# A trainium kernel's tensor-engine order in three mixers: a planner with lanes for the other engines, and high weight parts used before low

## The chip, the cores and the metric

The kernel runs on one core of a Trainium2 chip. The metric is the device time of one execution in microseconds (us); smaller is better. Engines are named as in the profile: PE (TensorE), DVE (VectorE), ACT (ScalarE), POOL (GpSimd), SP (SyncE, which here only issues transfers); "ACTq" and the like are the engines' queues of DMA issues.

## The reference, cut to what matters

512 tokens of 1024 features go through two blocks. The first block has two layers, each a "hybrid mixer" (a gated delta rule, forgetting attention, pooling) and then a feed-forward part: dense in layer 0, eight experts with two per token in layer 1. The second block mixes by RWKV-7 and an RG-LRU, and ends with cross attention on a memory and a convolutional feed-forward part.

```python
for layer in range(2):                                     # first block
    h = rmsnorm(x, norm1[layer])
    x = x + hybrid_mixer(h, w_in[layer], ..., w_out[layer])
    h = rmsnorm(x, norm2[layer])
    x = x + (swiglu(h, ...) if layer == 0 else moe_swiglu(h, router[0], ...))
...
h = rms_norm(x, norm_mix_g)                                # second block
proj = h @ w_in + b_in
y_a = rwkv7_branch(proj[..., :cb0], ...) @ w_branch_a      # chunked delta rule
y_b = rglru_branch(proj[..., cb0:cb1], proj[..., cb1:cb2], ...) @ w_branch_b
x = x + (sigmoid(proj[..., cb2:cg1]) * y_a + sigmoid(proj[..., cg1:]) * y_b) @ w_mix_out
x = x + cross_attention(rms_norm(x, norm_x_g), rms_norm(mem, norm_mem_g), ...)
x = x + conv_ffn(rms_norm(x, norm_ffn_g), ...)
return rms_norm(x, norm_final_g)
```

## The kernel before

By the trace the stages lie one after another: mixer 0 (0 to 340 us), dense feed-forward (to 674), mixer 1 (to about 1050, with the routing at its end), experts (to about 1712), the second block's mixer `mix2` (to about 2200), cross attention and the last feed-forward part (to 2720). Tokens lie along the free axis, features on partitions.

A dense product of two fp32 tensors is made of three fast products. A weight block `raw` is fetched on SP's queue; ACT rounds it to `whi`, DVE (or POOL, where the list of blocks says so) makes the rest `wlo`; activations are split in the same way (`xsh`, `xsl`). PE then adds high x high, high x low and low x high into one PSUM bank. In the three mixers `glin` does this for a block of eight 128-row pieces: before, piece by piece, in the order (whi,xsh), (whi,xsl), (wlo,xsh), with a point after each three at which another strand may go on. In the text a "dense row" is one such matmul.

The order of PE's instructions in the three mixers is found by `Fibers` when the program is built. Each strand of work is a generator ("fiber") with a rank: scans and normalisation have low ranks, `dense` has 3 and is the filler. At each `yield` a fiber says what it waits for: a number of us, a PSUM bank by name (`"pm"`, `"pf"`, `"px"`), or an event. `Fibers.run` steps its own clock by a cost for each matmul and takes the ready fiber of lowest rank; when a recent-load measure is low, all ranks from 2 up are taken before the rest. The order that it finds is kept on PE; PE then executes strictly in it, and waits wherever data are late. The other engines' order is made by the framework, and their times are in the planner only as the numbers written at the yields, `rel(tag, us)` (a bank comes free so long after now) and `done(us, name)`.

Places named later:

- `tinv` inverts the 64x64 triangular chunk matrices: 15 pairs of steps on DVE (`ipr`, `Tl`, L477 and L478), two 32x32 transposes on DVE (`T`, L481; `U`, L482), then chains of 32x32 matmuls on PE, of which `px<-T,MQ` is the first. Its waits before are `yield 0.9 + 0.006*i*i` for a step and 1.5 after the transposes.
- `rwkv(j)` of `mix2` prepares two heads: `G`, `BK`, `kk`, `rk` on DVE and POOL, and on PE `px<-G,BK` and the transposes `px<-cst,BK` (the last ones stand ahead of the inverse). `scan` then goes through eight chunks (`SV`), ends with a normalisation (`rr`, L1645) and the branch outputs `yah`, `yal`.
- `rstd` sums squares over partitions (`nacc`), takes a root on ACT, and spreads the result by `rdg`. In `mix2` it waits 14.0 us at its start.
- `conv` (L673, `cy`), `gates` (`gq`, `gsl`) and the bank evictions (`raw` L670, `pr` L1289, `MQ` L910) are DVE's part of the mixers' fronts; `attend` (`fF`, `fo`, `fP`) is the attention.
- `rows` (L1844) of mixer 1 turns the normalised tokens round (`px<-cst,xg`), copies them to `hTM` on ACT (L1858) and writes them to the DRAM buffer `hd` (L1861). `mem_k` beside it makes dense products of 256 columns (`pm<-msk,whi`) for the cross attention. The experts begin with POOL's gathers of rows of `hd` (`xa`, `xb`, L1936), which PE transposes (`px<-cst,xa`).

```python
    def rows(self):
...
                self.nc.scalar.activation(hT[:, 512 * b:512 * b + 512], ps, AF.Copy, scale=self.hrms[:, n:n + 1])
                F.rel("px", 0.8)
                yield 0.3
            self.nc.scalar.dma_start(self.hd[128 * n:128 * n + 128], hT)
```

## Time and profile before

| | |
|---|---|
| runs | 2723.54, 2724.38, 2728.06 us; median 2724.38 us |
| profiled execution | 2721.48 us, of which the trace's span is 2719.6 us |
| PE busy | 2586.2 us, 95% of the span |
| DVE, ACT, POOL busy | 1576.6, 1124.7, 374.2 us |
| mean granted PE clock | 0.974 |

PE is the busiest engine by far, so what another engine does costs time only where PE waits for it. A view by stages shows where PE is not busy; a view of waits says for whom; a timeline of one engine shows when the thing waited for was made. The granted clock is given as a share of full speed: 1.00 is 2.4 GHz, and the lower level is 1.2 GHz, so that a stretch with 0.9 had a part of its time at the lower level.

### The profile page before, as it was taken

What the parts mean: (1) busy time and instruction counts of PE and PEld (TensorE: products, weight loads), DVE (VectorE), ACT (ScalarE), POOL (GpSimd) and SP (SyncE); (2) the same over time, 40 slices, a digit from 0 to 9 for tenths busy, and PEclk for the clock granted to TensorE, in tenths of its full rate; (3) what the DMA queues carried; (4) which work ended last, traced back from release to release, by engine and by line L of the source; (5) the groups of instructions that cost most, each with busy time, mean ns of one, the idle gap of its engine ahead of it and who ended that gap; (6) DMA issues with size and microseconds to landing.
All of it is one profiled execution on the core that took longest, in us unless ns stands there. A gap on an engine that the chain in (4) does not pass through costs nothing.

```text
span 2719.6 us, 43763 instructions
## 1 busy us (share of the span) xinstructions
PE 2586.2 (95%) x18022; PEld 1996.7 (73%) x18022; DVE 1576.6 (58%) x2263; ACT 1124.7 (41%) x1600; POOL 374.2 (14%) x294
## 2 busy tenths in 40 slices
PE   7999999999989998999999998799989999999997
PEld 6787788888878667777777776566666676788885
DVE  5856643434585655666666665566743644544554
ACT  5344422223434434555555554464322334433232
POOL 4332000000333311000000001143432000000000
PEclk9999999999999999999999999899989999999998
DMA  3111222223312226787777776423232521222222
GB/s 115 55 57 43 91 92 95 93 93 101 102 55 64 72 80 250 249 297 277 278 269 266 263 254 227 135 67 108 84 115 88 173 90 43 93 94 93 93 93 79
DMA packets 101424, 359.38 MB, mean 132 GB/s; under 512 B 12256, under 2 KB 15712, under 8 KB 101216
## 3 DMA queue, kind: packets, MB, share of 16 engines
q1 hardware_dynamic: 82656, 308.47, 34.0%
q0 software_dynamic: 7808, 26.22, 2.8%
q10 hardware_dynamic: 10752, 21.81, 2.2%
q8 instruction: 144, 2.36, 0.4%
q14 instruction: 64, 0.52, 0.1%
HBM read 331.28 MB, written 25.17 MB: 131 GB/s over the span
## 4 chain that ended last, share of the span: by engine, by line
PE 55%; DVE 8%; DMA 3%; issue 3%; ACT 2%; POOL 0%; ACTq 0%; DVEq 0%; POOLq 0%; SPq 0%
PE pm L278 34%; PE pf L278 10%; PE px L278 10%; DMA raw<-in_s_gu_dram 1%; PE px L282 1%; DVE ipr L477 1%; DVE wl L1962 0%; DVE cy L673 0%; DVE G L1519 0%; PE pf L282 0%; ACT wh L1961 0%; DMA ye<-y 0%; DVE wlo L398 0%; DVE Tl L478 0%; DVE SV L1613 0%
## 5 line engine op out<-in xcount | busy, mean ns | idle before, releaser
L396 ACT ACTIVATE whi<-raw 128x1024 fp32r<-128x1024 f32 (+5 forms) x310 | 302.7, 977 | 797.2 <-PE pm L278 575.2
L278 PE MATMUL pm<-xsh,whi 128*128 128x512 f32 x1280 | 531.5, 415 | 12.3 <-ACT xsh L371 6.5
L278 PE MATMUL pm<-xsh,wlo 128*128 128x512 f32 x1280 | 511.9, 400 | 2.7 <-POOL wlo L398 2.6
L278 PE MATMUL pm<-xsl,whi 128*128 128x512 f32 x1280 | 512.3, 400 | 1.3 <-DVE xsl L372 1.3
L1962 DVE TENSOR_TENSOR wl<-raw,wh 128x1536 fp32r<-128x1536 f32 (+1 forms) x224 | 341.5, 1528 | 193.1 <-PE pf L278 85.8
L1961 ACT ACTIVATE wh<-raw 128x1536 fp32r<-128x1536 f32 (+1 forms) x224 | 291.3, 1305 | 256.8 <-PE pf L278 118.1
L278 PEld LDWEIGHTS pm<-xsh,whi 128*128 128x128 f32 x1280 | 245.2, 192 | 89.2 <-issue 19.4
L398 DVE TENSOR_TENSOR wlo<-raw,whi 128x1024 fp32r<-128x1024 f32 (+5 forms) x236 | 257.5, 1092 | 64.8 <-ACT whi L396 64.4
L278 PEld LDWEIGHTS pm<-xsh,wlo 128*128 128x128 f32 x1280 | 244.5, 191 | 62.9 <-POOL wlo L398 5.0
L278 PEld LDWEIGHTS pm<-xsl,whi 128*128 128x128 f32 x1280 | 245.3, 192 | 60.2 <-issue 4.5
L398 POOL TENSOR_TENSOR wlo<-raw,whi 128x1024 fp32r<-128x1024 f32 x74 | 181.1, 2447 | 359.7 <-ACT whi L396 359.7
L278 PE MATMUL pm<-hidl,whi 128*128 128x512 f32 x352 | 138.9, 395 | 0.0
L278 PE MATMUL pm<-hidh,wlo 128*128 128x512 f32 x352 | 138.6, 394 | 0.0
L278 PE MATMUL pm<-hidh,whi 128*128 128x512 f32 x352 | 137.9, 393 | 0.0
L1210 DVE TENSOR_TENSOR X<-X,pm 128x512 f32<-128x512 f32 x48 | 33.0, 688 | 135.1 <-PE pm L278 135.1
L278 PE MATMUL pf<-raw,xs 128*32 128x384 f32 x1024 | 103.2, 496 | 0.0
L278 PE MATMUL pm<-wh,xh 128*128 128x384 f32 x256 | 92.0, 370 | 7.4 <-ACT wh L1961 6.0
L278 PE MATMUL pm<-wl,xh 128*128 128x384 f32 x256 | 88.0, 345 | 3.6 <-DVE wl L1962 3.5
L278 PE MATMUL pf<-wh,xl 128*128 128x384 f32 x256 | 86.1, 337 | 0.0
L278 PE MATMUL pm<-wh,xl 128*128 128x384 f32 x256 | 86.0, 337 | 0.0
L278 PE MATMUL pf<-wl,xh 128*128 128x384 f32 x256 | 85.8, 336 | 0.0
L278 PE MATMUL pf<-wh,xh 128*128 128x384 f32 x256 | 84.6, 336 | 0.0
(606 smaller groups left out, 4697.5 us busy)
## 6 DMA issues: line engine op xcount, KB each, us to landing
raw<-in_s_gu_dram SPq DMA_DIRECT2D x128, 768.0 KB, 6.3
raw<-in_s_dn_dram SPq DMA_DIRECT2D x96, 512.0 KB, 4.4
raw<-in_f_gu_dram SPq DMA_DIRECT2D x44, 512.0 KB, 3.7
raw<-in_b_gu_dram SPq DMA_DIRECT2D x44, 512.0 KB, 3.7
raw<-in_b_wi_dram SPq DMA_DIRECT2D x38, 512.0 KB, 3.9
raw<-in_wq_dram SPq DMA_DIRECT2D x28, 512.0 KB, 3.6
raw<-in_f_dn_dram SPq DMA_DIRECT2D x16, 512.0 KB, 3.6
raw<-in_b_dn_dram SPq DMA_DIRECT2D x16, 512.0 KB, 3.6
```

Of the source, the lines that this page charges most:

```text
L278: return self.nc.tensor.matmul(o, l, r, **k)
L282: return self.nc.tensor.transpose(o, a, i)
L396: nc.scalar.activation(hi, raw, AF.Copy)
L398: (eng or nc.vector).tensor_tensor(lo, raw, hi.bitcast(F32), op=ALU.subtract)
L477: nc.vector.tensor_tensor(pr, A_, T_, op=ALU.mult)
L1210: nc.vector.tensor_tensor(self.X[m], self.X[m], ps, op=ALU.add)
L1961: self.wmark = act(hi, raw, AF.Copy)
L1962: tt(lo, raw, hi.bitcast(F32), op=ALU.subtract)
```

## The change

Only the planner's numbers and the order inside `glin` are changed; the work is the same.

- `Fibers` gets a lane (a list of taken intervals) for DVE, ACT, POOL, SP and the transfers. `Watch` and `Engines` stand between the kernel and the engines, and enter each instruction on its lane with a cost by its size, after its inputs are ready and its output buffer is free. A matmul waits on the planner's clock for its inputs.
- A number at a `yield` no longer counts: any number but 0 now means "until the last work that this fiber gave to another engine is done", a transfer's landing included. `rel` and `done` take their times in the same way. A list of tiles at a `yield` waits for these. `rstd` so waits for its input `acc` itself.
- Matmuls get other costs, by type and shape.
- `glin` now issues all (whi,x high) and (whi,x low) pairs of a block first, and then the low parts in groups of two, with a point for other strands after each group only.

```diff
     def set(self, lat, *k):
-        self.event(*k).t = self.t + lat
+        if self.cur is None:
+            return
+        self.event(*k).t = max(self.t, self.cur[4]) if lat else self.t
 
     def rel(self, tag, lat=1.0):
-        self.banks.setdefault(tag, []).append(self.t + lat)
+        if self.cur is None:
+            return
+        read = self.cur[5].get(tag)
+        t = self.used[read.pop(0)] if read else self.cur[4]
+        self.banks.setdefault(tag, []).append(max(t, self.t) + self.SEM)
...
+    def place(self, lane, t, cost):
+
+        iv = self.lanes[lane]
+        k = len(iv)
+        while k and iv[k - 1][0] > t:
+            k -= 1
+        if k and iv[k - 1][1] > t:
+            t = iv[k - 1][1]
+        while k < len(iv) and iv[k][0] < t + cost:
+            t = max(t, iv[k][1])
+            k += 1
+        iv.insert(k, (t, t + cost))
...
+    def work(self, lane, cost, outs, ins, land=0.0):
+
+        t = max([self.ready.get(i, 0.0) for i in ins] +
+                [max(self.ready.get(o, 0.0), self.used.get(o, 0.0)) for o in outs] + [0.0])
+        e = self.place(lane, t, cost)
+        if land:
+            e += land
...
+        if self.cur:
+            self.cur[4] = max(self.cur[4], e + self.SEM)
...
             try:
                 w = next(f[2])
-                f[3] = w if isinstance(w, (Event, str)) else self.t + w
+                f[3] = w if isinstance(w, (Event, str, list)) else max(self.t, f[4]) if w else self.t
...
+class Watch:
+
+    FIX = {"DVE": (0.155, 0.00104), "ACT": (0.19, 0.00084), "POOL": (0.35, 0.002)}
...
+        if "dma_start" in op:
+            n = int(np.prod(out.shape)) * 4
+            F.work(self.lane, {"ACT": 0.33, "SP": 0.33, "POOL": 0.56}[self.lane], [], ins)
+            F.work("DMA", n / 290e3, outs, ins, 1.7)
+            return
+        n = max(int(np.prod(x.shape[1:])) for x in every)
+        fix, per = self.FIX[self.lane]
+        if self.lane == "DVE":
+            per *= {"reciprocal": 6, "tensor_tensor_scan": 2}.get(op, 1)
+        elif "accum_out" in k:
+            fix += 0.19
+        F.work(self.lane, fix + per * n, outs, ins)
...
     def glin(self, ps, w, acts, first=True, last=True):
+
         n = len(acts)
+        yield list(w[:1])
         for k, a in enumerate(acts):
-            self.mm3(ps, [(w[0][:, k], w[1][:, k], a[0], a[1])], first and k == 0, last and k == n - 1)
+            yield list(a)
+            self.acc(ps, [(w[0][:, k], a[0]), (w[0][:, k], a[1])], first and k == 0, False)
+        yield list(w[1:])
+        for k in range(0, n, 2):
+            self.acc(ps, [(w[1][:, j], acts[j][0]) for j in range(k, min(k + 2, n))], False, last and k + 2 >= n)
             yield 0
...
         def rstd():
-            yield 14.0
+            yield [acc]
             st["R"], _ = yield from self.rstd_(acc)
```

What the change moves on PE is shown at three places; rows ending in x8 or the like stand for so many matmuls.

**The inverse of `mix2`**, PE, before: the start of `tinv`'s matmuls (`T32` is the `T` of the text). Ahead of the first row stand 141 dense rows, and ahead of these the last transposes of `BK`.

```order
L278 MATMUL px_17524<-T32_17511,MQ_16316 32x32 x32
L278 MATMUL px_17559<-T32_17511,MQ_16618 32x32 x4
L278 MATMUL pm_17501<-xsh_15352,whi_17459 128x512
L278 MATMUL pm_17501<-xsl_15353,whi_17459 128x512
L278 MATMUL pm_17501<-xsh_15352,wlo_17462 128x512
L278 MATMUL pm_17501<-xsh_15356,whi_17459 128x512
L278 MATMUL pm_17501<-xsl_15357,whi_17459 128x512
L278 MATMUL pm_17501<-xsh_15356,wlo_17462 128x512
L278 MATMUL pm_17501<-xsh_15360,whi_17459 128x512
L278 MATMUL pm_17501<-xsl_15361,whi_17459 128x512
L278 MATMUL pm_17501<-xsh_15360,wlo_17462 128x512
L278 MATMUL px_17559<-T32_17511,MQ_16618 32x32 x24
```

The same place of the changed kernel; ahead of the first row stand 82 dense rows, back to the same transposes of `BK`.

```order
L357 MATMUL px_17441<-T32_17411,MQ_16293 32x32 x32
L357 MATMUL pm_17432<-xsh_15340,whi_17389 128x512
L357 MATMUL pm_17432<-xsl_15341,whi_17389 128x512
L357 MATMUL pm_17432<-xsh_15344,whi_17389 128x512
L357 MATMUL pm_17432<-xsl_15345,whi_17389 128x512
L357 MATMUL pm_17432<-xsh_15348,whi_17389 128x512
L357 MATMUL pm_17432<-xsl_15349,whi_17389 128x512
L357 MATMUL px_17482<-T32_17411,MQ_16595 32x32 x24
L357 MATMUL pm_17432<-xsh_15352,whi_17389 128x512
```

The inverse has moved forward past 58 of the dense rows counted from the mixer's start (from 858 to 800), and the filler between its small matmuls comes in groups of six, where it had nine. Within the whole inverse 46 dense rows are now strewn, where it was 36; the dense rows left over stand in the scan and behind it.

**The end of mixer 1**, PE, before: the routing's counts (`rsm`, `oh`), the last of the eight groups of token transposes (`xg`), and the first of the 153 rows of `mem_k` that follow up to `px<-cst,xa` of the experts.

```order
L278 MATMUL px<-rsm,oh 128x8 x8
L278 MATMUL px<-rsm,oh 32x8 x8
L282 MATMUL px<-cst,xg 128x128 x4
L278 MATMUL pm<-msk_8566,whi 128x256
L278 MATMUL pm<-msk_8567,whi 128x256
L278 MATMUL pm<-msk_8566,wlo 128x256
```

The changed kernel, from shortly before its last group of token transposes to the first transposes of the experts.

```order
L357 MATMUL pm<-msk_8461,whi 128x256
L357 MATMUL pm<-msk_8531,whi 128x256
L357 MATMUL pm<-msk_8532,whi 128x256
L361 MATMUL px<-cst,xg 128x128 x4
L357 MATMUL pm<-msk_8531,whi 128x256
L357 MATMUL pm<-msk_8532,whi 128x256
L357 MATMUL pm<-msk_8401,wlo 128x256 x2
L357 MATMUL pm<-msk_8412,wlo 128x256 x2
L357 MATMUL pm<-msk_8460,wlo 128x256 x2
L357 MATMUL pm<-msk_8531,wlo 128x256 x2
L361 MATMUL px<-cst,xa 128x128 x8
L361 MATMUL px<-cst,xb 128x32 x8
```

Before, seven of the eight groups stood three rows apart and were out 153 rows ahead of the experts. Now the groups stand 8, 28, 8, 28, 10, 26 and 10 rows apart, and from the last to the experts there are ten rows.

**The normalisation at the front of `mix2`**, PE, before: 90 dense rows stand ahead of `nacc`, and 12 between it and `rdg`.

```order
L278 MATMUL pf<-xsh,wlo 128x512
L278 MATMUL px<-cst,nacc 128x1 x4
L278 MATMUL pf<-xsh,whi 128x512
L278 MATMUL pf<-xsl,whi 128x512
L278 MATMUL pf<-xsh,wlo 128x512
```

The changed kernel, where 30 dense rows stand ahead of `nacc`.

```order
L357 MATMUL pm<-xsl,whi 128x512
L357 MATMUL pm<-xsh,wlo 128x512 x8
L357 MATMUL px<-cst,nacc 128x1 x4
L357 MATMUL px<-rdg,cst 128x512
L357 MATMUL pm<-xsh,whi 128x512
L357 MATMUL pm<-xsl,whi 128x512
```

The root's input is now summed 60 dense rows sooner, and no row is left between `nacc` and `rdg`. In mixers 0 and 1 the same strand moved from 82 to 49 dense rows after the start, with twelve still between the two.

## Rows read from the trace of the kernel before

**Rows 1.** Windows by stage: busy us (instructions) of PE, PEld, DVE, ACT, POOL; PEclk; DMA.

```profile
0.00:340.00 340.00, 308.91 (x3053) 249.20 (x3054) 222.94 (x428) 152.11 (x294) 95.65 (x75) 0.97 0.23 72
340.00:674.00 334.00, 334.00 (x1441) 270.92 (x1440) 142.04 (x166) 90.13 (x106) 0.00 (x0) 1.00 0.29 94
674.00:1050.00 376.00, 354.08 (x3285) 282.22 (x3284) 230.71 (x469) 160.49 (x308) 110.32 (x87) 0.95 0.26 82
1712.00:2200.00 488.00, 447.13 (x3741) 328.79 (x3740) 286.57 (x424) 194.64 (x284) 136.73 (x96) 0.95 0.34 106
```

**Rows 2.** Waits of PE, 1712 to 2200: waited for: us in total, times, longest.

```profile
PE px L278 <- issue: 8.8, 6, 2.7
PE px L278 <- DVE G L1520: 7.8, 8, 2.6
PE px L278 <- DVE SV L1613: 3.5, 4, 1.7
PE pm L278 <- POOL wlo L398: 2.6, 4, 0.9
```

**Rows 3.** Timeline of PE around the inverse of mix2 (start, us, line).

```profile
1968.83 0.86 PE L278 MATMUL px<-cst,BK 64*64 64x64 f32 x22
...
2006.95 0.82 PE L278 MATMUL px<-T,MQ 32*32 32x32 f32 x72
```

**Rows 4.** Timeline of DVE before the inverse of mix2.

```profile
1987.11 2.22 DVE L481 STREAM_TRANSPOSE T<-Tl 128x1024 f32<-128x1024 f32 x1
...
1989.81 1.98 DVE L482 STREAM_TRANSPOSE U<-Tl 128x1024 f32<-128x1024 f32 x1
```

**Rows 5.** Timeline of PE at the normalisation of mix2.

```profile
1751.82 0.95 PE L278 MATMUL px<-cst,nacc 128*128 128x1 f32 x8
...
1755.51 1.02 PE L278 MATMUL px<-rdg,cst 128*128 128x512 f32 x2
1757.94 0.50 PE L278 MATMUL pm<-xsh,whi 128*128 128x512 f32 x1 [1.41 <-DVE pr L1289]
```

**Rows 6.** Timeline of ACT in the gates of mixer 0.

```profile
42.31 1.28 ACT L818 ACT_TABLE_LOAD   x1
```

**Rows 7.** Windows of the attention in mixer 1.

```profile
900.00:960.00 60.00, 54.25 (x426) 38.44 (x425) 37.89 (x95) 32.35 (x82) 14.27 (x20) 0.91 0.26 82
```

**Rows 8.** Timeline of PE at the end of mixer 1.

```profile
1042.95 0.66 PE L282 MATMUL px<-cst,xg 128*128 128x128 f32 x4 [0.32 <-DVE tokens L1834]
...
1064.68 1.03 PE L282 MATMUL px<-cst,xa 128*128 128x128 f32 x8
```

**Rows 9.** Timeline of ACT after it.

```profile
1043.64 0.69 ACT L1858 ACTIVATE hTM<-px,rtm 128x512 f32<-128x512 f32 x1 [3.26 <-PE px L282]
...
1046.21 0.39 ACTq L1861 DMA_DIRECT2D hd<-hTM  x1
```

**Rows 10.** Timeline of POOL: the first gather.

```profile
1050.26 1.26 POOL L1936 DMA_INDIRECT xa<-hd,tokens  x1 [23.51 <-DVE mK L1906]
```

**Rows 11.** The tile xa: from issue to landing.

```profile
DMA to landing us min/median/max: 5.0/5.6/12.8
```

**Rows 12.** Windows at the end of mixer 1.

```profile
1020.00:1064.60 44.60, 39.53 (x292) 37.48 (x292) 23.35 (x66) 16.58 (x22) 6.46 (x6) 0.89 0.57 193
1050.00:1064.60 14.60, 13.92 (x118) 13.93 (x119) 7.13 (x9) 3.18 (x4) 3.97 (x4) 1.00 0.89 293
```

**Rows 13.** Waits of PE, 20 to 340 us.

```profile
PE px L278 <- DVE MQ L910: 4.4, 2, 3.6
PE px L278 <- DVE T L481: 1.9, 1, 1.9
```

**Rows 14.** Timeline of DVE, one operation twice, in rwkv.

```profile
1856.32 3.01 DVE L1519 SCALAR_TENSOR_TENSOR G<-kk,EE 64x504 f32<-64x504 f32 x1
...
1859.44 0.68 DVE L1519 SCALAR_TENSOR_TENSOR G<-kk,EE 64x504 f32<-64x504 f32 x1
```

**Rows 15.** Timeline of POOL in the same stretch.

```profile
1856.40 2.38 POOL L398 TENSOR_TENSOR wlo<-raw,whi 128x1024 fp32r<-128x1024 f32 x1
```

More of the change, by code (lines that the diff above doesn't have):

```diff
@@ L24 @@
 NEG = -1.0e30
+DBG = 0
 EPS = 1e-6
@@ L193 @@
 class Fibers:
-    DENSE, LO, HI = 2, 1.1, 1.5
+    DENSE, LO, HI, SEM = 2, 1.1, 1.5, 0.06
     def __init__(self, banks):
         self.t, self.n, self.q = 0.0, 0, []
-        self.heat = self.cols = self.idle = 0.0
+        self.heat = self.cols = self.idle = self.stall = 0.0
         self.tick, self.warm, self.low = 3.413, False, True
         self.banks = {k: [0.0] * v for k, v in banks.items()}
-        self.ev = {}
+        self.ev, self.ready, self.used, self.bank = {}, {}, {}, {}
+        self.lanes = {k: [] for k in ("DVE", "ACT", "POOL", "SP", "DMA")}
+        self.cur, self.plain = None, False
     def event(self, *k):
@@ L208, in set, with free, use @@
     def set(self, lat, *k):
-        self.event(*k).t = self.t + lat
+        if self.cur is None:
+            return
+        self.event(*k).t = max(self.t, self.cur[4]) if lat else self.t
     def rel(self, tag, lat=1.0):
-        self.banks.setdefault(tag, []).append(self.t + lat)
+        if self.cur is None:
[3 more added lines that the diff above has]
+        self.banks.setdefault(tag, []).append(max(t, self.t) + self.SEM)
     def add(self, gen, rank=0):
         self.n += 1
-        self.q.append([rank, self.n, gen, 0.0])
-    def use(self, us, rows):
+        self.q.append([rank, self.n, gen, 0.0, 0.0, {}])
+    def free(self, old, new):
+        self.ready[new] = max(self.ready.get(old, 0.0), self.used.get(old, 0.0))
+    def place(self, lane, t, cost):
[9 more added lines that the diff above has]
+        iv.insert(k, (t, t + cost))
+        if len(iv) > 400:
+            del iv[:200]
+        return t + cost
+    def work(self, lane, cost, outs, ins, land=0.0):
[4 more added lines that the diff above has]
+            e += land
+        for i in ins:
+            self.used[i] = max(self.used.get(i, 0.0), e)
+            if i in self.bank and self.cur:
+                read = self.cur[5].setdefault(self.bank[i], [])
+                if i not in read:
+                    read.append(i)
+        for o in outs:
+            self.ready[o] = e + self.SEM
+        if self.cur:
+            self.cur[4] = max(self.cur[4], e + self.SEM)
+    def use(self, us, rows, plain, outs, ins):
+        w = max([self.ready.get(i, 0.0) for i in ins] + [0.0]) - self.t
+        if w > 0:
+            self.stall += w
+            self.heat *= math.exp(-w / 1.7)
+            self.pass_(w)
+        if plain != self.plain:
+            us += 0.1 if plain else 0.24
+            self.plain = plain
         d = max(us * (1 if self.warm else 2), 0.036)
@@ L223, in use @@
         self.pass_(d)
+        for i in ins:
+            self.used[i] = max(self.used.get(i, 0.0), self.t)
+        for o in outs:
+            self.ready[o] = self.t + 0.2
     def pass_(self, d):
@@ L237, in _ready @@
             return min(b) if b else None
+        if isinstance(w, list):
+            return max(self.ready.get(tid(a), 0.0) for a in w)
         return w
@@ L267, in __init__, with _cost @@
         self.nc, self.F = nc, None
[L269 to L274 removed]
+    def _cost(self, o, l, r, c=4):
+        if not self.F:
+            return
+        n, m, k = int(np.prod(r.shape[1:])), int(np.prod(l.shape[1:])), r.shape[0]
+        plain = r.dtype == F32
+        if not plain:
+            ns = n * 0.453
+        else:
+            ns = n * c * 0.419
+            if k <= 32 and m <= 32:
+                ns *= 0.57
+            elif k <= 64:
+                ns *= 0.65 if n <= 64 else 0.58
+            elif m <= 64:
+                ns *= 0.89 if n <= 64 else 1.25
+            else:
+                ns = max(ns * 1.05, 54.0 * c)
+        self.F.use(ns / 1000, k / 128, plain and (k < 128 or m < 128), [tid(o)], [tid(l), tid(r)])
@@ L285, with __init__, __getattr__ @@
+class Engines:
+    def __init__(self, nc, pe):
+        self._nc = nc
+        self.vector, self.scalar = Watch(nc.vector, "DVE", pe), Watch(nc.scalar, "ACT", pe)
+        self.gpsimd, self.sync = Watch(nc.gpsimd, "POOL", pe), Watch(nc.sync, "SP", pe)
+    def __getattr__(self, n):
+        return getattr(self._nc, n)
 class Net:
     def __init__(self, tc, es, A, po):
-        self.tc, self.nc, self.A, self.po = tc, tc.nc, A, po
+        self.tc, self.A, self.po = tc, A, po
         self.pe = Tensor(tc.nc)
-        self.F = Fibers({})
+        self.nc = Engines(tc.nc, self.pe)
+        self.F, self.slots = Fibers({}), {}
@@ L690, in dense @@
                 pv.append(self.ps(tag)[:, :402])
-            yield from self.tm(2, get, acts, pv, at=lambda b, n: (b, n) == (3, 0) and done(1.5, "acc"))
+            yield from self.tm(2, get, acts, pv)
             g["pv"] = pv
@@ L1120, in mixer @@
             F.run()
+        print('model', F.t, 'idle', F.idle, 'stall', F.stall) if DBG else None
         self.pe.F = None
@@ L1127, in tm @@
             hi, lo = get()
+            yield [hi, lo]
             for n in range(len(outs)):
@@ L1282, in rstd @@
         def rstd():
-            yield 14.0
+            yield [acc]
             st["R"], _ = yield from self.rstd_(acc)
@@ L1677, in mix2 @@
             F.run()
+        print('model', F.t, 'idle', F.idle, 'stall', F.stall) if DBG else None
         self.pe.F = None
```

58 lines of the change are left out of this document (43 added, 15 removed).

## The prediction

> **What bounds the kernel now.** I read the windows by stage first. In the dense feed-forward stage PE is busy for all of its 334.00 us, with 1441 matmuls: 0.232 us for a dense row of 512 columns. In the three mixers it is not: 340 − 308.9 = 31 us idle in mixer 0, 376 − 354.1 = 22 in mixer 1, and 488 − 447.1 = 41 in mix2; the granted clock there is 0.97, 0.95 and 0.95 [rows 1]. So at most some 94 us of idle time, and what the lower clock costs, lie in the planner's reach; the rest is matmuls whose number doesn't change. A part of the 31 us is the start, where the first weights must arrive; no order helps there.
>
> The waits of PE say for whom it stands in mix2: 7.8 us for `G`, 3.5 for `SV` of the scan, 2.6 for low parts that POOL makes, and 8.8 us for nothing that the profile shows [rows 2]. Many short waits, none of them large.
>
> The other thing to see is the reverse of a wait: PE coming late to what is ready. In mix2 the last `BK` transposes start at 1968.83 and the inverse's first matmul at 2006.95 [rows 3], but DVE had `T` ready at 1987.11 + 2.22 = 1989.3, and `U` at 1989.81 + 1.98 = 1991.8 [rows 4]. The dependent chain (inverse, scan, tail) starts 15 us later than it could, and behind it filler runs short.
>
> **The change, part by part.** *The inverse of mix2.* 58 dense rows leave the stretch ahead of it: 58 × 0.232 = 13.5 us. PE would arrive at 2006.95 − 13.5 = 1993.5, 1.7 us after `U`, so the move makes no new wait by itself. It is no gain either: the 58 rows are still to be done. They pay where they stand in what was idle: in the inverse (10 more rows, 2.3 us), in the scan and its tail (48 rows, 11.1 us). Bounds: nothing, if they only push the chain along, and 13.5 us, if each finds a hole. The named holes behind the inverse are `SV`'s 3.5 us and a part of the 8.8 without a releaser; the larger ones are the half-clock stretches, which this view does not price. I take 8, above the middle, since the scan's chunks had nine dense rows each in the order and now have twelve.
>
> *The heads of mix2.* Between a head's lora product and its first `px<-G,BK` there were 33 dense rows four times; now there are 32, 36, 42 and 40. For the later three that is up to 3 + 9 + 7 = 19 rows or 4.4 us of cover, against 7.8 us of waits [rows 2]. Between 0 and 4.4 I take 3.
>
> *Low parts last.* With `wlo` used 16 rows (3.7 us) after its `whi`, instead of two, the 2.6 us for POOL's low parts [rows 2] have cover; the longest wait was 0.9. I take the whole 2.6; the low bound is nothing, if the high parts now wait instead.
>
> *The normalisation of mix2.* Before, `nacc` and `rdg` start 1751.82 and 1755.51, with twelve dense rows between them [rows 5]; now none. A table load of ACT, of which the gates of mixer 0 show one, is 1.28 us [rows 6], and the root needs one, so PE must stand between 1.28 and 1755.51 − 1751.82 = 3.7 us. I take 3, nearer to the upper end since three short operations follow the load, and give back the wait of 1.41 us for `pr`'s bank that stood right behind `rdg` [rows 5]: a loss of 1.6.
>
> Mix2 together: −8 − 3 − 2.6 + 1.6 = −12.0 us.
>
> *Attention of mixer 1.* Here PE idles 60 − 54.25 = 5.75 us, and the clock is 0.91 [rows 7], because the filler ran out. The scan starts 21 dense rows (4.9 us) earlier, and filler lasts through. Bounds 0 and 5.75; I take 4.
>
> *The end of mixer 1: a loss.* Before, the last `xg` transposes start at 1042.95, and the experts' first transposes at 1064.68 [rows 8]. In between runs a chain that nobody sees, since 153 rows of `mem_k` cover it: ACT's copy starts at 1043.64 and takes 0.69; its write `hd` is issued only at 1046.21 [rows 9], on a queue where `kd` stood before it; POOL's gather `xa` starts at 1050.26 [rows 10], 4.05 us after that issue; and a gather's landing takes 5.0 us at least, 5.6 in the median, 12.8 at most [rows 11]. From the last `xg` that makes 1.38 (to the end of the copy) + 0 to 1.88 (the queue) + 4.05 + 5.0 to 12.8 = 10.4 to 20.1 us; with 0.4 for the queue and 5.6 for the landing 11.4. Now only ten rows stand in this place, at 13.92 us for 118 of them [rows 12] 1.2 us. So 9.2 to 18.9 us lie open, most likely 10.2. PE is in order: all that follows waits. What comes back: in the 44.6 us up to the experts PE was idle 44.6 − 39.5 = 5.1 us [rows 12], mostly among the token transposes, which are now strewn with 8 to 28 rows between them. I give back 2.2 of it: a loss of 8 (4 to 19). The planner puts them so because `yield 0.3` in `rows` now waits for a landing on its clock, and it has no event from `hd` to the gathers.
>
> *The fronts of mixers 0 and 1.* `nacc` comes 33 dense rows earlier, 7.7 us, and the strands behind it too. In mixer 0 PE waited 4.4 us for `MQ` and 1.9 for `T` [rows 13]; these can go, and others come, since DVE's operations are not faster than before and PE gets to their results sooner. Without a row that decides, I take −2 for mixer 0 (it has the most idle time) and 0 for mixer 1, each with ±6.
>
> **The sum.** −12.0 − 4 + 8 − 2 = −10.0 us. The profiled execution took 2721.48 us (2719.6 of span and 1.9 around it): 2711.5. The median of the runs shown is 2.9 above it, and by that I say 2714. Against what a measurement of this kernel tells from no change, 0.2% or 5.4 us, that is faster, by not much.
>
> **The rivals.** *Lanes hurt: slower.* The lanes price a DVE instruction by its size alone. The trace shows the same `G` operation at 3.01 us and at 0.68 [rows 14]; beside the slow one POOL makes a low part, 2.38 us [rows 15]. So a planner that counts 0.68 puts PE's next step 2.33 us too early wherever such a pair meets on the chain. The place is the fronts: the inverse stands 27 rows of 256 columns earlier in mixer 0 and 51 in mixer 1, 3.2 and 6.0 us by the 0.118 us of such a row, and PE waits there for `T` already [rows 13]. If DVE's chain does not come forward, that is +9.2; with three stretched steps on it (+7.0) it outweighs the −10.0 and the time is 2724.4 − 10.0 + 16.2 = about 2731. From three such steps on this decides. For it: the mixers are where POOL works at all (96 and 110 us against 0 in the dense stage) [rows 1]. Against it: the old order, with times set by hand, has the same stretches, and DVE's work is not longer than it was. The Trainium skill ("SBUF — State Buffer", section "Who interferes with whom") says that a DVE instruction with two inputs in SBUF and a GpSimd instruction that reads SBUF take turns on a shared port pair, the later one blocked until the other ends. The trace agrees: 0.68 + 2.38 = 3.06, where 3.01 was measured. By that rule this rival is a fixed property of the lanes, not chance.
>
> *More comes than I count.* If a third of the 94 us goes, as a planner that sees all chains might bring, and the experts' start costs no more than 4, the time is 2724.4 − 31 + 4 = about 2697. For it: the low clock, which I price at nothing, has 0.05 × 488 = 24 us at full speed in mix2 alone [rows 1]. Against it: 8.8 us have no releaser, and the start of mixer 0 can't be filled.
>
> *Nothing is gained.* The stalls change their places only: filler that stands in the scan is missing elsewhere, mix2 gains some 6 instead of 12 and the experts' start takes it back: 2724.4 ± 5.4.
>
> **How the numbers follow.** The forecast, −6 to −16 us, has 0.43; more 0.14; nothing 0.19; slower 0.24. So faster 0.57, same 0.19, slower 0.24. The forecast's own range is 2708 to 2718. Eight in ten need both signs: from 2694, near the larger gain, to 2735, a little above the slower rival, since the experts' start alone can cost 11 us more than I took.
>
> **What would show it.** In the windows of the changed kernel mix2's idle time falls from 41 to about 30 us, and its inverse starts at once after `U`. In front of the first `px<-cst,xa` PE waits some 10 us, with POOL's gather the thing waited for. Waits for POOL's `wlo` are gone. In the front of mix2 one wait of about 3 us stands ahead of `rdg`. I am wrong if PE's waits for `T`, `kF` or `gq` in mixers 0 and 1 add up to more than 15 us; if `T` and `U` in mix2 come later than PE; or if the experts' start is covered after all, because the transposes come out earlier relative to the gathers than I count.

## The result

The changed kernel takes 2801.59 us (median of four runs, 2798.34 to 2804.74) against 2723.96 us before: 1.0286 times, with a 95% interval of 1.0273 to 1.0298. It is 78 us slower, where 10 us less were forecast, and lies 67 us above 2735, the upper end of the eight-in-ten range (84 us above the forecast's own 2718).

The windows view of the changed kernel, by stages (busy us and instructions of PE, PEld, DVE, ACT, POOL; granted clock; DMA). The third row ends at the experts' start, where [rows 1] ended 15 us sooner; the profiled execution took 2804.74 us, with a span of 2802.9.

```profile
0.00:374.00 374.00, 322.42 (x3055) 258.01 (x3056) 224.44 (x428) 153.83 (x294) 95.89 (x75) 0.93 0.21 65
374.00:708.00 334.00, 334.00 (x1441) 270.82 (x1440) 142.40 (x167) 90.44 (x107) 0.00 (x0) 1.00 0.29 94
708.00:1140.00 432.00, 377.51 (x3402) 302.99 (x3401) 239.58 (x478) 167.38 (x312) 114.21 (x91) 0.91 0.28 89
1786.00:2281.00 495.00, 449.80 (x3745) 329.26 (x3746) 281.00 (x429) 199.40 (x286) 134.86 (x96) 0.94 0.33 108
```

The reader is to see three things beside [rows 1]. The dense stage is the same: PE does the same 1441 matmuls in a window of 334 us and is busy throughout. Mixer 0 takes 374 us instead of 340 with practically the same matmuls (3055 against 3053); its idle time went from 31.1 to 374 − 322.4 = 51.6 us, and its busy time rose by 13.5 us too, because the clock fell from 0.97 to 0.93 (308.9 x 0.97 and 322.4 x 0.93 are both about 300). Mixer 1 up to the experts takes 432 us; before, the same work lay between 674 and 1064.68 [rows 1, 8], 391 us. Mix2, 495 against 488, has some 7 us of the loss, but 5 of them lie ahead of its first dense row, which stands 19.3 us behind the window's start, before 14.4. So 34 + 41 us lie in the two mixers for which I had set −2 − 4 + 8.

Mixer 0 in three parts of the changed kernel: the front up to the inverse's first matmuls, the inverse and the scan, and the attention.

```profile
0.00:160.00 160.00, 121.36 (x914) 100.16 (x915) 99.38 (x165) 58.59 (x88) 56.46 (x38) 0.88 0.22 72
160.00:251.00 91.00, 88.80 (x1554) 73.82 (x1553) 52.09 (x126) 41.21 (x103) 23.81 (x20) 1.00 0.19 60
251.00:301.00 50.00, 43.29 (x226) 30.63 (x226) 29.07 (x68) 22.09 (x56) 15.62 (x17) 0.93 0.07 20
```

The front of the kernel before, for the first of these rows:

```profile
0.00:160.00 160.00, 132.72 (x1278) 111.64 (x1279) 109.84 (x181) 65.34 (x104) 62.00 (x40) 0.94 0.26 82
```

The numbers of matmuls in these two rows can't be compared as they stand: the kernel before had begun its inverse at 142.6, and 304 of the 1278 are small matmuls on 32 partitions, where it is 56 of the 914. Counted in the traces, PE now does 384 dense rows in the first 160 us, where it did 500; it is idle for 38.6 us instead of 27.3, and the clock is 0.88 instead of 0.94. DVE, whose work all this waits for, does not get more done by PE's coming earlier: it is busy 99 us where it was 110.

For whom PE stands in mixer 0 of the changed kernel (us in total, times, longest):

```profile
PE px L357 <- ACT hsq L379: 6.8, 2, 4.4
PE pf L361 <- DVE fP L379: 5.7, 4, 4.7
PE pf L357 <- DVE wlo L379: 4.4, 1, 4.4
PE px L357 <- DVE kF L379: 4.4, 2, 4.2
PE px L357 <- DVE vF L379: 4.3, 2, 3.5
PE px L357 <- DVE ipr L379: 3.7, 1, 3.7
PE pm L357 <- DVE rdg L379: 3.0, 1, 3.0
```

Before, the largest were `MQ`, 4.4 [rows 13], and these two:

```profile
PE pf L278 <- DVE wlo L398: 4.4, 1, 4.4
PE px L278 <- DVE kF L666: 3.3, 1, 3.3
```

The 4.4 us for `wlo` is the same wait near the start in both kernels. The others are now waits of 3 to 7 us for each strand's next step. How one of them comes about is seen at the first `kF`. DVE, at that place:

```profile
50.07 2.41 DVE L379 COPY fxt<-nck 128x8 f32<-128x8 f32 x1
...
52.39 0.68 DVE L379 TENSOR_TENSOR raw<-pm,Rbc 128x512 f32<-128x512 f32 x1
53.94 3.95 DVE L379 SCALAR_TENSOR_TENSOR cy<-raw,par,cy 128x511 f32<-128x511 f32 x3 [0.87 <-ACT cy L379]
58.65 0.69 DVE L379 SCALAR_TENSOR_TENSOR kF<-th,cy 128x512 f32<-128x512 f32 x1 [0.76 <-ACT th L379]
```

POOL, beside it:

```profile
50.05 2.40 POOL L379 TENSOR_TENSOR wlo<-raw,whi 128x1024 fp32r<-128x1024 f32 x1
52.41 1.04 POOL L379 TENSOR_TENSOR gm<-gh,cst 128x512 f32<-128x512 f32 x1
```

PE, which had been sent for `kF`:

```profile
54.27 1.03 PE L357 MATMUL pm<-xsh,wlo 128*128 128x512 f32 x2
59.49 0.80 PE L357 MATMUL px<-cst,kF 64*64 64x64 f32 x10 [4.19 <-DVE kF L379]
```

POOL begins a low part at 50.05 that takes 2.40 us; a copy of eight columns on DVE takes 2.41 beside it; only then is the block's bank emptied (`raw`, 52.39), and `conv`'s three steps take 3.95 us together, 1.32 each, beside POOL's next operations (`kF`, a step of the same kind and size, takes 0.69 when POOL is idle). `raw`, which reads a bank in PSUM, keeps its 0.68 though POOL works. PE stands 4.19 us for `kF`. All dense rows behind this point wait with it, and these are what the next `raw`, `cy` and `vF` are made of.

In mix2 the inverse of the changed kernel: `T` and `U` on DVE, and the first of PE's matmuls for it.

```profile
2076.83 2.21 DVE L379 STREAM_TRANSPOSE T<-Tl 128x1024 f32<-128x1024 f32 x1
...
2079.51 1.98 DVE L379 STREAM_TRANSPOSE U<-Tl 128x1024 f32<-128x1024 f32 x1
```

```profile
2082.79 0.75 PE L357 MATMUL px<-T,MQ 32*32 32x32 f32 x64
```

PE comes 1.3 us after `U` (2079.51 + 1.98), as forecast. But from the stage's start (1786 for 1712) `U` is ready at 295.5, where it was at 279.8 [rows 4], 15.7 us later. Of these, 5 lie ahead of mix2's first dense row; from that row on (1805.28 for 1726.35) the chain itself is 10.8 us later. PE comes to the inverse only 3.1 us sooner, for the 13.5 us of the 58 rows taken from ahead of it, and from there to the last output product it needs 5.5 us more than before (195.1 for 189.6). PE is idle for 495 − 449.8 = 45.2 us, where I expected about 30. Some of the waits of mix2:

```profile
PE pm L357 <- DVE wlo L379: 6.4, 4, 2.9
PE pm L357 <- DVE pr L379: 6.1, 4, 1.7
PE pf L357 <- ACT ksq L379: 5.4, 4, 2.8
PE px L357 <- DVE xx L379: 4.1, 3, 1.9
PE px L357 <- DVE rdg L379: 1.6, 1, 1.6
PE px L357 <- DVE G L379: 0.8, 1, 0.8
```

`G` is down from 7.8 [rows 2] to 0.8 and POOL's low parts are gone, as I said; `rdg` costs 1.6 where I had 3. The table load that I had put between `nacc` and `rdg` starts at 1818.04, ahead of `nacc` at 1819.90 (before at 1750.05, ahead of 1751.82), and isn't in PE's wait. In their place stand DVE's `wlo`, more of `pr`, and `ksq` and `xx` (the keys' norm, and the branch with the RG-LRU), 22.0 us in the first four rows, of which `wlo` and `pr` had 1.2 and 3.7 before.

The start of the experts, on PE, ACT and POOL of the changed kernel:

```profile
1125.33 1.10 PE L357 MATMUL pm<-msk,wlo 128*128 128x256 f32 x8
1140.03 1.94 PE L361 MATMUL px<-cst,xa 128*128 128x128 f32 x8 [13.59 <-DMA xa<-hd,tokens]
```

```profile
1125.29 0.69 ACT L379 ACTIVATE hTM<-px,rtm 128x512 f32<-128x512 f32 x1 [2.81 <-PE px L361]
1126.01 0.33 ACTq L379 DMA_DIRECT2D hd<-hTM  x1
```

```profile
1130.52 1.04 POOL L379 DMA_INDIRECT xa<-hd,tokens  x1 [41.57 <-DMA hd<-hTM]
```

This is the chain of [rows 8 to 11] laid open: the last copy at 1125.29, the write at 1126.01, the gather at 1130.52 (4.51 us after; before 4.05), its data 9.4 us later (1139.89). PE waits 13.59 us.

### The profile page after: what moved, and what is told of

Read it like the earlier page. It is cut to its first block, busy times and chain, and to the rows that moved or that the text cites. A ratio compares the mean times of both kernels' runs of the same rounds, so it can differ in the third digit from the quotient of the medians.

```text
span 2802.9 us, 43777 instructions
## 1 busy us (share of the span) xinstructions
PE 2614.0 (93%) x18022; PEld 2015.6 (72%) x18022; DVE 1570.6 (56%) x2263; ACT 1134.3 (40%) x1602; POOL 372.7 (13%) x294
## 5 line engine op out<-in xcount | busy, mean ns | idle before, releaser
L357 PE MATMUL pm<-xsh,whi 128*128 128x512 f32 x1280 | 529.4, 414 | 14.4 <-ACT xsh L379 6.2
L357 PE MATMUL pm<-xsh,wlo 128*128 128x512 f32 x1280 | 451.2, 405 | 0.0
L357 PEld LDWEIGHTS pm<-xsh,whi 128*128 128x128 f32 x1280 | 247.8, 194 | 83.2 <-issue 13.5
L379 DVE TENSOR_TENSOR X<-X,pm 128x512 f32<-128x512 f32 x96 | 66.0, 687 | 218.8 <-PE pm L357 218.8
L379 DVE TENSOR_TENSOR tu<-pm,Rbc 128x512 f32<-128x512 f32 x44 | 30.4, 691 | 127.4 <-PE pm L357 127.4
L379 POOL TENSOR_TENSOR nacc<-nacc,nsq 128x512 f32<-128x512 f32 x21 | 30.6, 1456 | 516.1 <-ACT nsq L379 515.6
L379 DVE TENSOR_TENSOR tg<-pm,Rbc 128x512 f32<-128x512 f32 x44 | 30.4, 692 | 106.8 <-PE pm L357 104.3
```

The source lines that it names most:

```text
L357: return self.nc.tensor.matmul(o, l, r, **k)
L379: return f(*a, **k)
```

## The experiments

Each kernel was run with the kernel before on the same chip; ratios are to that. The table has the places in the traces that the text speaks of, in us: mixer 0's first inverse matmul (T), its scan's start and the last row of its output projection, from the span's start; the same output row and the experts' first transposes, from the end of the dense stage; and the last output product of mix2 from the experts' last product.

| kernel | ratio (95%) | m0 T | m0 scan | m0 output | m1 output | experts | mix2 |
|---|---|---|---|---|---|---|---|
| before | 1 | 142.6 | 190.2 | 327.1 | 324.1 | 366.8 | 540.5 |
| changed | 1.0286 | 158.7 | 203.9 | 355.4 | 353.6 | 408.5 | 547.9 |
| new planner in mix2 alone | 1.0003 (0.9991 to 1.0016) | 143.9 | 191.6 | 330.1 | 324.6 | 366.7 | 543.7 |
| old order of parts, lanes | 1.0229 (1.0205 to 1.0253) | 154.9 | 200.1 | 349.3 | 346.8 | 399.8 | 552.5 |
| low parts last, no lanes | 1.0024 (1.0010 to 1.0038) | 139.7 | 187.3 | 326.8 | 324.0 | 363.2 | 546.0 |
| POOL and tables priced | 1.0247 (1.0223 to 1.0271) | 156.2 | 201.9 | 340.3 | 341.1 | 395.5 | 559.1 |
| transposes without the wait | 1.0242 (1.0219 to 1.0264) | 156.0 | 201.3 | 352.4 | 353.5 | 404.4 | 545.7 |
| hand's times as floor | 1.0153 (1.0124 to 1.0183) | 142.7 | 192.3 | 339.7 | 335.4 | 391.8 | 541.5 |
| lane prices x 1.5 | 1.0118 (1.0091 to 1.0145) | 153.2 | 196.3 | 328.1 | 324.2 | 377.2 | 556.3 |
| DVE's prices x 1.5 | 1.0170 (1.0146 to 1.0195) | 180.0 | 217.2 | 339.2 | 334.8 | 385.2 | 562.1 |
| lanes in strict order | 1.0117 (1.0093 to 1.0140) | 156.4 | 201.2 | 335.1 | 329.8 | 384.3 | 539.0 |
| before, hand's times x 0.5 | 1.0329 (1.0313 to 1.0345) | 143.7 | 198.6 | 366.0 | 358.9 | 405.8 | 554.4 |
| before, hand's times x 1.5 | 1.0005 (0.9993 to 1.0017) | 153.7 | 197.8 | 325.6 | 316.6 | 357.2 | 552.4 |
| all mended | 1.0045 (1.0031 to 1.0060) | 152.6 | 195.6 | 328.3 | 323.9 | 374.9 | 536.9 |
| old planner, strict lanes in mix2 | 0.9987 (0.9976 to 0.9999) | 142.7 | 190.4 | 328.9 | 320.8 | 362.2 | 540.0 |
| the same, old order of parts | 1.0026 (1.0015 to 1.0037) | 141.7 | 187.8 | 326.3 | 323.9 | 366.4 | 552.4 |
| before, x 1.5 in mixers 0 and 1 | 0.9950 (0.9938 to 0.9962) | 153.5 | 197.6 | 325.5 | 316.5 | 357.0 | 539.8 |
| the same, strict lanes in mix2 | 0.9948 (0.9936 to 0.9960) | 156.1 | 200.2 | 328.0 | 316.9 | 358.6 | 539.7 |

Each row of places is one execution. Rows whose matmuls stand in the same order differ by up to 4.6 us (mixer 0's output 326.3 to 330.1 in the four with the old planner's order there, the experts' start 362.2 to 366.8), so a smaller difference between two rows may be chance.

**Where it is lost.** A second planner of the old kind stands beside the new one, and the two mixers take it.

```diff
-        F = self.F = self.pe.F = Fibers({"pm": 2, "pf": 3, "px": 3})
+        F = self.F = self.pe.F = Hand({"pm": 2, "pf": 3, "px": 3})
```

> Mixers 0 and 1 are planned as before the change (their matmuls stand in the old order), mix2 as after it. By the two traces mixer 0 lost 33.6 us, mixer 1 with the routing 41.7 us, and mix2 some 6 us. If the losses belong to their stages and add up: 2724 + 6 = about 2730 us. Rival: mix2 gains alone what I forecast for it (12 us) and only starts late in the changed kernel because its buffers and weights come late from before: about 2712.

2724.08 us against 2722.05: no difference, with an interval from 2 us less to 4 us more. The change to mix2 alone costs and gives nothing that can be told from this; the 78 us are lost in mixers 0 and 1, with mixer 1's end.

**The two halves of the change.** First the lanes with the old order of parts, then the new order of parts under the old planner.

```diff
-            self.acc(ps, [(w[0][:, k], a[0]), (w[0][:, k], a[1])], first and k == 0, False)
...
+            self.mm3(ps, [(w[0][:, k], w[1][:, k], a[0], a[1])], first and k == 0, last and k == n - 1)
```

> The changed planner with the old order of parts in each dense block (high, high x low, low x high, piece by piece). Theory L (the lanes price the other engines too cheaply, so PE is sent to data that are late): the order inside the blocks is not what costs, 2790 to 2810 us. Theory G (using low parts last makes the blocks longer, holds banks longer and ruins the filler): most of the 78 us comes back, 2725 to 2750.

> The kernel before with the new order inside the dense blocks alone (high parts first, then low), under the old planner. Undoing this order in the changed kernel gave 13 us back. If it costs by itself (a block's last matmuls then wait for nothing but its bank is held as long, and the filler comes in other pieces): 2730 to 2738 us. Rival: it costs only together with the lanes, where the waits for whi and wlo are planned: 2720 to 2727.

The new planner with the old order of parts: 2788.57 us, 62 us over the kernel before by the ratio, 67 by the medians. The loss is the new planner's: lanes, waits and costs of matmuls together, which no run takes apart. The order of parts has 13 of the 78 us in the changed kernel. Alone in the old kernel it costs 2727.76 against 2722.18, 1.0024 times or 6 us; I had put it down as a gain of 2.6. In its trace 5.5 us are lost in mix2 and 5.0 between mixer 0's output and the end of the dense stage. The 5.0 us stand in every run that has low parts last in mixer 0 (375.6 to 376.4 us for this stretch) and in none with the old order (370.7 to 371.1): before, five rows of the dense stage's first block stand between `nacc` and `rdg` there, with low parts last none, so that PE waits 3.0 us for `rdg` where it was 0.3, and the clock over the 20 us around it is 0.83 where it was 1.00. In mix2 the order has no fixed price: see the end of this section.

**Two prices that the lanes lack.** A DVE operation (a copy, or an operation on a tensor with a scalar or a second tensor) without an operand in PSUM waits on the planner's clock until POOL is idle; ACT pays for a new table.

```diff
+        if lock and lane == "DVE":
+            t = self.clear(t, cost)
         e = self.place(lane, t, cost)
...
+            if f in ("Exp", "Ln", "Sqrt", "Gelu_apprx_tanh", "Silu") and f != F.table:
+                F.table, fix = f, fix + 1.28
```

> The changed kernel, but on the planner's clock a DVE operation with no operand in PSUM waits until no POOL operation runs, and ACT pays 1.28 us when it changes its function table. Theory L: the front is planned nearer to what happens, and PE's extra waits for kF, hsq, vF and the T step shrink: 2740 to 2770 us. Rival (what is missing in the lanes is not these two prices, but the order in which the engines really take their work, or the loss of the margins written by hand): 2785 or more.

2791.1 us: about 10 of the 78 us. In mixers 0 and 1 the outputs came 15.1 and 12.5 us sooner, in mix2 the end came 11 us later. Up to mixer 0's output PE is idle for 37.3 us, where it was 47.9 in the changed kernel (30.1 before), but the largest waits are nearly as long as they were, some for other strands:

```profile
PE px L373 <- POOL nacc L395: 5.2, 1, 5.2
PE px L373 <- DVE ipr L395: 4.7, 1, 4.7
PE px L373 <- ACT hsq L395: 4.2, 1, 4.2
PE px L373 <- DVE MQ L395: 4.2, 1, 4.2
```

So my rival's mechanism can be a part of it, but no more; this run priced tables along with the stretch and doesn't part the two. Pricing what is known to be missing did not make the plan fit.

**The transposes at the experts' start.**

```diff
                 F.rel("px", 0.8)
-                yield 0.3
+                yield 0
```

> The changed kernel with one yield of the token transposes (rows) put back to no wait, so that they no longer wait for a transfer's landing on the planner's clock. By the trace the experts' start lost 12 us more than the part ahead of it (29.5 late at the output projection, 41.7 at the experts). If the strewn transposes are the cause: 2788 to 2794 us. Rival: the chain is as long, and other work only takes its place: 2798 to 2802.

2791.2 us: 10 us. By the table 4 of them lie at this place (from mixer 1's output to the experts 50.9 us, for 54.9 in the changed kernel; the four with the old order have 41.4 to 42.7) and 3 in mixer 0, whose order is the same. Between the last transposes and the experts there are 112 rows now instead of ten, and still PE waits 9.42 us. ACT's last write, POOL's gather, and PE:

```profile
1113.08 0.39 ACTq L379 DMA_DIRECT2D hd<-hTM  x1
```

```profile
1122.24 1.04 POOL L379 DMA_INDIRECT xa<-hd,tokens  x1 [36.30 <-DMA raw<-in_s_gu_dram]
```

```profile
1132.92 1.94 PE L361 MATMUL px<-cst,xa 128*128 128x128 f32 x8 [9.42 <-DMA xa<-hd,tokens]
```

The write is out at 1113.08, the gather follows at 1122.24, 9.2 us later where it was 4.05 before, and its data come 10.7 us after that. In the 9.2 us the transfers moved 369 GB/s, in the 4.3 before the gather of the kernel before 183, in the changed kernel's 4.5 it was 229. So the chain was longer where more was being moved, the experts' weights among it; that the one makes the other is not shown by a run of its own. The yield explains 4 of the 12 us.

**Margins.** The hand's times come back as a floor under the lanes; then the lanes' prices are raised; then the filling of gaps is taken out.

```diff
-                f[3] = w if isinstance(w, (Event, str, list)) else max(self.t, f[4]) if w else self.t
+                f[3] = w if isinstance(w, (Event, str, list)) else max(self.t + w, f[4]) if w else self.t
```

> The changed kernel, but the numbers written by hand at the yields, at rel and at done count again as a floor: the planner's clock takes the later of the lane's end and the hand's time. Theory M (the hand's numbers held the margin that a fixed order needs, the lanes hold none): a good part of the 78 us comes back, 2740 to 2770. Rival (the new order of the fronts itself, normalisation first and strands as early as possible, is what costs): 2785 or more, since gq, hsq and the T step hardly move (378 rows ahead of T in both).

> The changed kernel with every price of a DVE, ACT and POOL operation on the lanes multiplied by 1.5: 510 dense rows stand ahead of mixer 0's T step, where it was 405 before and 378 after the change. Theory M: PE comes late enough to find its data, the waits in the fronts go, 2735 to 2765 us. Rival: the chain is late anyhow (DVE does its work no sooner), and filler spent in front is missing in the attention: 2785 or more.

> The changed kernel with the lanes' prices multiplied by 1.5 for DVE alone. With 1.5 on all three engines it was 2754.8. If DVE's price is the one that is short (it is the engine whose operations stretch beside POOL): 2750 to 2770 us. Rival (ACT's or POOL's chains are as short): 2775 or more.

```diff
-        while k and iv[k - 1][0] > t:
...
-        iv.insert(k, (t, t + cost))
+        if iv and lane != "DMA":
+            t = max(t, iv[-1][1])
+        iv.append((t, t + cost))
```

> The changed kernel with lanes that take work strictly in the order in which it is issued, with no filling of gaps (transfers excepted): 495 rows ahead of T. If the filling of gaps is what makes the lanes too hopeful: 2740 to 2765 us. Rival (prices, not order): 2785 or more.

2764.04, 2754.79, 2774.98 and 2754.9 us, in this order: each way of making the planned times longer takes back 27 to 47 of the 78 us, none all. With all prices x 1.5 the outputs of both mixers are where they were before (328.1 and 324.2 against 327.1 and 324.1); what is left of its loss stands behind mixer 0's output (5, with low parts last), at the experts' start (10 us) and in mix2 (16). So the new costs of matmuls, which are still in it, are not what loses the mixers' time. DVE's price alone takes back a little over half as much (27 of 47).

**The margin without any lanes.** In the kernel before, only the numbers at the yields, `rel` and `done` are scaled.

```diff
-        self.event(*k).t = self.t + lat
+        self.event(*k).t = self.t + 0.5 * lat
...
-                f[3] = w if isinstance(w, (Event, str)) else self.t + w
+                f[3] = w if isinstance(w, (Event, str)) else self.t + 0.5 * w
```

> The kernel before, no lanes, old order inside the blocks; only every time written by hand at a yield, rel or done is halved on the planner's clock. Theory M (a fixed order loses when its planned times fall short of the real ones, whoever gives them): clearly slower, 2745 to 2800 us, with the loss in mixers 0 and 1, in the waits for kF, hsq, vF, T and in the attention. Rival (the loss comes from other features of the new planner: its banks, its costs of matmuls, its lists): 2715 to 2735.

> The kernel before with every time written by hand multiplied by 1.5 on the planner's clock, the counterpart of the halved ones (2813.8). If it is coming too early that costs, and coming too late is covered by filler while filler lasts: at most a third of the +91, 2715 to 2750 us. Rival (any departure from the tuned times costs alike): 2780 or more.

2813.84 us with halved times, 2724.66 against 2724.54 with times half as long again. The old planner loses 91 us when its times are halved, and the whole stays as it was when they are half as long again. By the table (of the fastest of ten runs, 2716.74 us) the latter hides two effects: the experts begin 9.6 us sooner, and mix2 loses 12; mixer 0's 1.5 us are less than executions differ by. The front of mixer 0 and PE's waits in it, with halved times:

```profile
0.00:160.00 160.00, 117.32 (x990) 94.63 (x991) 100.11 (x159) 57.27 (x86) 54.75 (x37) 0.87 0.21 69
```

```profile
PE px L278 <- DVE T L481: 6.6, 1, 6.6
PE px L278 <- DVE ipr L477: 5.0, 1, 5.0
PE px L278 <- DVE kF L666: 4.8, 2, 2.9
PE px L278 <- DVE Q L666: 4.0, 1, 4.0
PE pf L282 <- DVE fxt L733: 3.8, 1, 3.8
```

This is the picture of the changed kernel without any of its code: 332 dense rows in 160 us (of the 990 matmuls 288 are small ones of the inverse), clock 0.87, and many strands waited for. With the longer times:

```profile
0.00:160.00 160.00, 135.18 (x1201) 115.53 (x1201) 114.24 (x187) 68.74 (x111) 66.15 (x42) 0.95 0.27 86
```

```profile
PE px L278 <- DVE KB L925: 7.0, 1, 7.0
PE pm L278 <- POOL wlo L398: 2.9, 2, 2.3
```

567 dense rows, clock 0.95, two waits of note beside the 4.4 us for `wlo` near the start, although T stands 11 us later than before. The traces of mixer 0, counted in dense rows, have both sides:

| kernel | rows ahead of T | PE idle up to T, us | rows behind the attention |
|---|---|---|---|
| before, hand's times x 0.5 | 279 | 42.7 | 273 |
| changed | 378 | 38.6 | 212 |
| before | 405 | 27.3 | 177 |
| lane prices x 1.5 | 510 | 26.2 | 120 |
| before, hand's times x 1.5 | 531 | 24.8 | 120 |
| DVE's prices x 1.5 | 672 | 25.5 | 134 |

With fewer rows ahead of the inverse than before PE stands idle, and the rows are found again behind the attention; with more the idle time stays at some 25 us. In the last row too much was moved ahead: between the inverse's start and the scan's only 48 rows are left (234 before), PE is idle there for 7.9 us, and the output is 12 us late.

**Mended, and faster.** Three mends of the changed kernel in one: prices x 1.5 in mixers 0 and 1, strict lanes in mix2, no wait in the transposes.

> The changed kernel with three mends: prices of the lanes times 1.5 in mixers 0 and 1, lanes in strict order at their own prices in mix2, and no wait for a landing in the token transposes. By the traces of the single mends: mixer 0 +4, mixer 1 to the experts +6 (10 less 4), mix2 -1.5 against the kernel before, 2728 to 2734 us. If the three causes are not separate, 2740 or more.

2736.21 against 2724.54 us. Of the 78 us some 12 remain. In the trace (2731.14 us, the fastest of the five) mixer 0 and the `rdg` behind it have 6 (5 of them the price of low parts last at this place), the experts' start 8, and mix2 is 3.6 shorter than before, which is within what executions differ by. Then mix2 by strict lanes with the old planner in mixers 0 and 1, with the new and with the old order of parts:

> Mixers 0 and 1 as before the change; mix2 by the changed planner with lanes that take work strictly in order (the trace with such lanes everywhere had mix2's scan and tail end 5 us sooner and its last product 1.5 us sooner than before). If the stages add up: 2718 to 2722 us, against 2722 before on the same chip: no difference or barely one. Rival: the gain in mix2 came from what stands ahead of it, 2724 to 2728.

> As the kernel with in-order lanes in mix2 alone, with the old order inside the dense blocks there too. In the kernel before, low parts last cost 5.5 us in mix2 and gave nothing back. If that holds here: 2713 to 2718 us, the one version that would beat both kernels. Rival: with these lanes the low parts' waits come back (2.6 us for POOL's low parts before): 2720 to 2725.

2720.13 and 2729.54 us against 2722.78: 0.9987 (0.9976 to 0.9999) and 1.0026 (1.0015 to 1.0037). In its trace mix2 is only 0.5 us shorter than before. Low parts last is worth 9 us here, where it cost 5.5 in the old kernel's mix2: it depends on the plan around it. Last, the old kernel with the longer hand times in mixers 0 and 1 alone, and this with mix2 by strict lanes:

```diff
         F = self.F = self.pe.F = Fibers({"pm": 2, "pf": 3, "px": 3})
+        F.scale = 1.5
```

> The kernel before with the hand's times 1.5 times as long in mixers 0 and 1 alone. With 1.5 everywhere the trace had mixer 0 some 1.5 us and mixer 1 some 9.6 us sooner than before, and mix2 12 us later. If the stages add up: 2724 less 11, 2711 to 2716 us. Rival: what mixer 1 gains comes back later as a wait of the experts for their weights: 2720 to 2725.

> As the kernel with the longer hand times in mixers 0 and 1, and mix2 by the changed planner with lanes in strict order (alone 0.9987 of the kernel before). If both add up: 2707 to 2714 us, faster than both kernels. Rival: the gains do not add, 2717 to 2724.

2707.21 and 2707.63 us against 2721.42: 0.9950 (0.9938 to 0.9962) and 0.9948 (0.9936 to 0.9960). Both are faster than both kernels, than the one before by 14 us; the two gains don't add, since mix2 by strict lanes has hardly one (539.7 us for 539.8). The forecast for the first was 4 to 9 us too high. Of the other forecasts above, these lay outside every range named: mix2 alone, lanes alone (by 1.4 us), low parts last alone, DVE's prices x 1.5 (5 us above), halved times (14 above), all mended (2 above) and strict lanes with the old order of parts (12 above its range).

## Why the prediction was wrong

**The step that failed** is the last of the parts: "*The fronts of mixers 0 and 1.* ... I take −2 for mixer 0 (it has the most idle time) and 0 for mixer 1, each with ±6." Measured, mixer 0 lost 28 us and mixer 1 29.5 us up to their outputs. I had set old waits that go against new waits that come, each worth its own length. The runs show something else: up to the output PE's idle time in mixer 0 rose from 30.1 to 47.9 us, and the clock, 0.94 for 0.97, took the other 10.5. PE takes its list in order, so a step that stands too early holds back all filler behind it (4.19 us at the first `kF`), and that filler is also what the chain is fed with (the dense blocks of the next `conv`). The front came 13.7 us later to the scan although its steps stood earlier in the list, and the filler that could not be used in the front, with the lower clock between the waits, is found again behind the attention: 212 dense rows for 177, and other strands' matmuls, 14 us more (output 55.3 us after the attention's last product, 41.2 before). Halved hand times show that shorter planned times do this alone; longer ones show that the other side costs nothing in these two mixers, as long as there is filler, though it does in mix2. That the lanes' times fall short of the real ones is concluded from the runs in which longer ones gave time back; no run sets the planner's clock beside the trace. None of the three signs that I had named for being wrong came up: the waits for `T`, `kF` and `gq` add up to 6.9 us in both mixers, not to more than 15, since PE stood for `hsq`, `vF`, `fP` and `fF`.

**Attention of mixer 1** (−4): of the wrong sign. From the scan's start to the attention's last product PE is idle for 15.4 us, before 6.5, and 9.0 of it are for `fF`:

```profile
PE pf L361 <- ACT fF L379: 5.5, 1, 5.5
PE pf L357 <- ACT fF L379: 3.5, 1, 3.5
```

The filler didn't run out: 206 dense rows stand behind the attention, 177 before. That they stand there for the same reason as in mixer 0 is argued, not shown.

**The end of mixer 1** (+8, 4 to 19): right in place and kind. PE waits 13.59 us for the gather, the bound being 9.2 to 18.9, and the part lost 408.5 − 353.6 less 366.8 − 324.1, 12.2 us. Too small was the gather's landing: I took 5.6 us, the median over all experts, and the first gather took 9.4; at this place it had taken 6.6 in the kernel before too, and its neighbours up to 12.8.

**Mix2** (−12): `G`, POOL's low parts, a wait at `rdg` (1.6 us, not 3) and PE's arrival right behind `U` came as written, and the stage still lost 7 us in the profile (2 from its first dense row on) and nothing in the run with this part alone. The sum held the start of DVE's chain fixed while it moved PE; `U` was 10.8 us later, counted from the first dense row. DVE's low parts took back what POOL's had given: 6.4 us of waits for 1.2.

**The rival "lanes hurt"** had the right sign, the right place and a cause that may have a part in it, POOL beside DVE. Its price was wrong: three stretched steps and 16 us, where pricing the stretch, with the tables, gave back 10 of 78. It is not shown which further shortfalls of the lanes make up the rest; the runs show that halving the times of a plan without lanes costs as much (91 us), and that the filling of gaps is a part of it. As the lanes were mended in three places 12 us remained, of which 8 stand at the experts' start.

## What to carry to other kernels

A fixed order on the bound engine is not symmetric: a step that stands too late costs little as long as there is filler left to put beside it, and a step that stands too early stops the filler and the chain with it, once for each wait and again by the clock. So give a planner's times a margin before making them exact, and try the margin first, stage by stage: one factor on two stages gave 0.5% here, where the same factor cost mix2 12 us and a model of all engines lost 2.9%. When you judge a moved step, ask what feeds the chain that it waits for, and whether that stands behind it in the same queue.

## What was not expected of the hardware

A copy of 128 x 8 on DVE took 2.41 us beside a 2.40 us operation on POOL (0.16 us at its shortest in the same kernel), so a DVE operation on eight columns in SBUF paid for a whole POOL operation, while `raw`, from PSUM, kept its 0.68. The Trainium skill ("SBUF — State Buffer", section "Who interferes with whom") counts copies among the DVE instructions that can take the port pair shared with GpSimd, and leaves out those with at most one input in SBUF outside such modes; both agree with these rows, and the lanes of the changed kernel know of neither. Which of the two stands back is not settled by the starts: in [rows 14, 15] the stretched DVE operation starts 0.08 us ahead of POOL's. The step from the write `hd` to the gather `xa` took 9.2 us at 369 GB/s, where it was 4.05 at 183 GB/s in the kernel before; the gather's data came 10.7 us later, where that took 6.6 to 12.8 at this place before. And PE's busy time for practically the same matmuls of mixer 0 (3055 for 3053) rose by 13.5 us with the clock's fall from 0.97 to 0.93, two thirds of what the waits themselves added (20.5).
